# The last quarter of an output projection, computed token-major instead of feature-major

## The chip, the cores and the metric

One NeuronCore of a Trainium2 chip runs the whole program. The metric is the device time of one execution in microseconds (us). TensorE (PE in the profile) multiplies, with its weight loads shown apart (PEld); VectorE is DVE, ScalarE is ACT, GpSimd is POOL, and SyncE (SP) issues most DMAs. Each of these works through its own queue in the order of its program.

## The reference

One decoder layer over 512 tokens of 2,048 features. The part around the change:

```
mix = (g_a * y_a + g_b * y_b) @ w_o[l]
x = x + gt_a * mix
h = _rmsnorm(x, norm_ffn[l]) * (1.0 + sc_f) + sh_f
gate, up = jnp.split(h @ w_gate_up[l], 2, axis=-1)
```

`gt_a`, `sc_f` and `sh_f` are vectors of 2,048 features. The norm needs the sum over all features of x squared for each token, so no column of `h` can be formed before the last quarter of `mix @ w_o` is in x.

## The kernel before, in words

Every float32 operand is kept as a rounded part ("hi") and the rest ("lo"), and each product takes three matmuls: hi by hi, hi by lo, lo by hi. Weights arrive by DMA as "raw" tiles of 128x1024; ScalarE casts each to hi (L270) and VectorE subtracts to get lo (L271). There are five buffers for hi and five for lo, so a cast must wait until TensorE is done with the unit of weights five places earlier.

The work is a list of units (`Unit`, L37), each a piece of weights and the matmuls that use it. `Driver.run` (L113) takes them in order and issues their matmuls. It also counts matmuls by weight, and each time 12 are counted (`GROUP`, L34) it pumps: each generator in `drv.chains` (a chain of follow-up work, such as an epilogue) takes one step. `yield n` in a chain skips n - 1 pumps. `drv.hold()` at the end of a set costs one pump. TensorE, GpSimd and SyncE keep the order in which the program issues. On VectorE and ScalarE the order is set by a scheduler when the program is built, and it is then as fixed as the others.

All matmuls are recorded under L157, so tiles name them. Four stages matter, in this order:

- **The w_o product.** Columns 1024 to 1535 (`wo2`) come first, feature-major: a weight piece is stationary and all 512 tokens move. Columns 0 to 1023 come next by a Strassen scheme (`strassen_wo`), token-major. Its `finish` (L1448) multiplies each 128x512 tile by a gate row, adds x, stores the sum to `z_dram`, transposes it on TensorE (`zT`), copies it out of PSUM with ScalarE (L1471) and adds its squares to a running sum (`squares`, L1335: a Square on ScalarE, an add on GpSimd or VectorE).
- **The last quarter** (`half_sets`, L1530, called at L1763), columns 1536 to 2047, feature-major in two halves of 256 tokens. The first half goes through all 16 rows of weight tiles, then the second half does so again with weights loaded and split anew. Each matmul has a 128x128 weight piece as stationary operand and 256 tokens moving. A unit is 24 matmuls; a half is 8 units, 192 matmuls. At a half's end `wo_half_done` (L1520) adds gate times PSUM to the feature-major x (four instructions of 128x256 for a half's two tiles, L1329), squares, and starts `turned_x2` (L1504), which transposes the sums (`x2T`) and stores them to `z_dram`.
- **The norm** (`h2_gen`, L1786), one chain per half of the tokens. `part_rstd` (L1345) reduces the sum of squares on TensorE (`hss`), takes the reciprocal root on VectorE (tiles `rs`, then `diag`), and `spread` brings it to all partitions on TensorE (`hbc`). Then for each of eight pairs of feature tiles (q = 0 to 7) VectorE scales (L1795, two instructions), ScalarE shifts (L1796, two), ScalarE casts (L244, `h2h`) and VectorE subtracts (L247, `h2l`). The chain of the first half is started at the end of the last quarter's first half; its `hss` stands after 32 matmuls of the second half.
- **The first part of w_gate_up** (`gu0`), token-major, again in two halves of 256 tokens. A unit is 12 matmuls of 512 columns and uses one q. The first half's 96 matmuls use q = 0 to 7 of the first half of tokens, and meanwhile the norm's chain for the second half runs: its `hss` stands after 28 of those 96 matmuls, its `hbc` after 64.

In what follows v0 to v7 are the units of the last quarter's second half, and g0 to g7 those of gu0's first half.

Of the kernel before, what the change touches and what calls it, by code (L numbers as in the profile page):

```python
# [12 lines left out]
ALU = mybir.AluOpType  # L13
AX = mybir.AxisListType

P = 128
# [3 lines left out]
KT = 16  # L20
# [153 lines left out]
def block_kernel(ctx: ExitStack, tc: tile.TileContext, a: dict, out):  # L174
    nc = Core(tc, PINNED)
# [16 lines left out]
    def S(s, dt=F32):  # L192
        return slots.tile([P, 512], dt, tag="s", name=nm(s))

    def PS(s):
        return psum.tile([P, 512], F32, tag="ps", name=nm(s))
# [4 lines left out]
    def load(dst, src):  # L201
        nc.sync.dma_start(dst, src)

    def side(dst, src):
        nc.gpsimd.dma_start(dst, src)
# [6 lines left out]
    def tok(j):  # L212
        return slice(j * P, (j + 1) * P)
# [784 lines left out]
    chains = {}  # L998
# [318 lines left out]
    def load_x2(qs):  # L1317
        for q in qs:
            for h in range(2):
                x2[h][q] = S("x2")  # L1320
                load(x2[h][q][:].rearrange("p (k n) -> p k n", k=2),
                     a["xT"][256 * q:256 * q + 256, 256 * h:256 * h + 256].rearrange("(k p) n -> p k n", p=P))
# [12 lines left out]
    def squares(q, seg, eng):  # L1335

        s = S("sq")
        st = sums.setdefault(seg, [])
        nc.scalar.activation(view(s, seg), view(x2[seg[0]][q], seg), AF.Square)
        if st and eng is not None:  # L1340
            eng.tensor_tensor(view(st[0], seg), view(st[0], seg), view(s, seg), ALU.add)
        else:
            st.append(s)
# [79 lines left out]
    def strassen_wo():  # L1423
# [69 lines left out]
        def back(h):  # L1493
            for f in range(2):
                for t in range(2):
                    xk[h, t, f] = S("xk")
                    load(xk[h, t, f][:], a["x"][0, P * (2 * h + t):P * (2 * h + t) + P, 512 * f:512 * f + 512])

        with_pre([us[9]], gates)
        with_pre([us[12]], lambda: back(0))  # L1500
        with_pre([us[14]], lambda: (back(1), load_x2((6, 7))))
        return us

    def turned_x2(h, n):  # L1504
# [15 lines left out]
    def wo_half_done(n):  # L1520
        def done(h, ps):
            for j in range(4):
                k = 4 * n + j
                add_gated(h, k, ps[j // 2][:, 256 * (j % 2):256 * (j % 2) + 256], gt_mix)
                if j % 2:
                    squares(k // 2, HALF[h], nc.vector)
            drv.add(turned_x2(h, n))
        return done

    def half_sets(name, loads, x, done):  # L1530

        st = [None, None]

        def unit(h, k0):
            box = {}

            def start():
                box["raw"] = fetch(loads(k0, 2), 512, 2)

            def split():  # L1540
                box["w"] = halves(box.pop("raw"), 512, 2)

            def pre():
                if k0 == 0:
                    st[h] = [PS(name) for _ in range(2)]

            def one(kk, j, n, wi, xi):
                k = k0 + kk
                mm(st[h][j // 2][:, 256 * (j % 2):256 * (j % 2) + 256], box["w"][wi][:, kk, tok(j)],
                   x(k)[xi][:, 256 * h:256 * h + 256], start=k == 0 and j % 2 == 0 and n == 0,  # L1550
                   stop=k == KT - 1 and n == 2, skip_group_check=True)

            mms = [lambda kk=kk, j=j, n=n, wi=wi, xi=xi: one(kk, j, n, wi, xi)
                   for kk in range(2) for j in range(4) for n, (wi, xi) in enumerate(((0, 0), (0, 1), (1, 0)))]

            def post():
                if k0 + 2 == KT:
                    done(h, st[h])
                    st[h] = None
                    drv.hold()  # L1560

            return Unit(start, split, mms, pre, post, alone=True)

        return [[unit(h, k0) for k0 in range(0, KT, 2)] for h in range(2)]
# [55 lines left out]
    def with_pre(units, fn):  # L1620
        u = units[0]
        p0 = u.pre

        def pre():
            fn()
            if p0 is not None:
                p0()
        u.pre = pre
        return units
# [30 lines left out]
    def mixing():  # L1660
# [99 lines left out]

        def more():
            drv.ahead = LOADS
        first, second = half_sets("wo3", lambda k0, nk: loads(k0, nk, 3), mv, wo_half_done(3))  # L1763

        def half0():
            drv.finish(chains["act"])
            start_h2(0)()
        yield from with_pre(first, more) + with_pre(second, half0)


    def half_of(tile_, k):
# [13 lines left out]

    def h2_gen(h):  # L1786

        yield 3 if h else 1
        diag = part_rstd([HALF[h]])
        yield 6 if h else 4  # L1790
        r = spread(*diag)
        for q in range(8):
            f = S("h2f")
            for k in (2 * q, 2 * q + 1):
                nc.vector.scalar_tensor_tensor(half_of(f, k), half_of(x2[h][q], k), s_ffn[:, k:k + 1], r, op0=ALU.mult, op1=ALU.mult)  # L1795
                nc.scalar.activation(half_of(f, k), half_of(f, k), AF.Identity, bias=sh_ffn[:, k:k + 1])  # L1796
            x2[h][q] = None
            h2f[h][q] = f
            h2T[h][q] = hilo(f[:], "h2")
            h2n[h] = 2 * q + 2  # L1800
            yield 2
# [821 lines left out]
```

## Time and profile before

| What | us |
|---|---|
| Median of three runs | 2712.14 |
| Lowest, highest of the three | 2709.2, 2715.04 |
| The profiled execution's own time | 2706.44 |
| Its span, first to last instruction | 2704.6 |
| Mean granted TensorE clock | 0.999 of full |
| TensorE busy | 2683.6 |
| VectorE busy | 2087.6 |
| ScalarE busy | 1201.6 |

How to read it: the profile is of one execution, so sums are made against its 2706.44 us, 5.70 us under the median. Matmuls are pipelined: the recorded length of one (0.28 or 0.39 us) is longer than the time from its start to the next start, and it is the latter that adds up. A row of the timeline gives start, length, engine, line, operation, output and inputs, the count where equal rows were merged, and in brackets the engine's idle time before it and what ended that.

### The profile page before, as it was taken

The page shows a single profiled execution, that of the slowest core. Times are in us where ns is not written, and L with a number is a line of the kernel's source. Part 1 is how long each engine was busy: PE and PEld are TensorE (multiplying, and loading weights), DVE is VectorE, ACT ScalarE, POOL GpSimd, SP SyncE. Part 2 cuts the span into 40 slices and gives each one's busy share as a digit, 9 for nine tenths or more (in the row PEclk, how much of TensorE's full clock was granted, in tenths as well). Part 3 has the DMA queues.
Part 4 walks back from the last instruction along what each step waited for, and adds up shares of the span by engine and source line. Part 5 has one row for each costly group of instructions (what it writes and reads, how often), then busy time and mean ns, then how long its engine had stood idle before and what let it go on. Part 6 is the DMA issues. An engine that isn't in the chain of part 4 may idle for free.

```text
span 2704.6 us, 36528 instructions
## 1 busy us (share of the span) xinstructions
PE 2683.6 (99%) x13046; PEld 2237.3 (83%) x13046; DVE 2087.6 (77%) x3230; ACT 1201.6 (44%) x1720; POOL 228.6 (8%) x310
## 2 busy tenths in 40 slices
PE   9999999999999999999999999999999999999998
PEld 7888788888888888888888888888888888888886
DVE  8785666777768866768788778788878888788786
ACT  3443432453245333234574444444444446545454
POOL 0000002011100000000010000001101101011012
PEclk9999999999999999999999999999999999999999
DMA  9897565646664867854763566567767777788595
GB/s 372 306 351 268 158 192 177 201 152 191 187 172 136 286 223 285 306 187 134 272 193 120 193 209 208 202 218 250 243 227 263 252 249 212 210 238 226 179 278 154
DMA packets 312126, 600.45 MB, mean 222 GB/s; under 512 B 42852, under 2 KB 69636, under 8 KB 311816
## 3 DMA queue, kind: packets, MB, share of 16 engines
q1 hardware_dynamic: 257160, 486.52, 54.7%
q0 software_dynamic: 21888, 59.83, 8.3%
q10 hardware_dynamic: 32896, 51.78, 5.2%
q8 instruction: 102, 1.67, 0.3%
q14 instruction: 80, 0.66, 0.1%
HBM read 507.80 MB, written 90.20 MB: 221 GB/s over the span
## 4 chain that ended last, share of the span: by engine, by line
PE 98%; DVE 1%; ACT 1%; issue 0%; DMA 0%; SPq 0%; DVEq 0%; ACTq 0%
PE m L157 43%; PE gb L157 6%; PE v L157 4%; PE z L157 3%; PE ya L157 3%; PE ga L157 3%; PE k L157 3%; PE s L157 3%; PE q L157 3%; PE yb L157 3%; PE wo L157 3%; PE gu L157 3%; PE dn L157 2%; PE qk L157 2%; PE dnt L157 2%; PE ckv L157 2%
## 5 line engine op out<-in xcount | busy, mean ns | idle before, releaser
L1888 ACT CAST hi<-raws 128x1024 fp32r<-128x1024 f32 (+1 forms) x360 | 322.9, 907 | 575.3 <-DVE raws L1868 346.9
L1895 DVE TENSOR_TENSOR lo<-raws,hi 128x1024 fp32r<-128x1024 f32 (+1 forms) x360 | 376.0, 1046 | 176.5 <-ACT hi L1888 168.9
L270 ACT CAST hi<-raw 128x1024 fp32r<-128x1024 f32 x262 | 271.9, 1041 | 489.8 <-DMA raw<-in_w_in_dram 130.7
L271 DVE TENSOR_TENSOR lo<-raw,hi 128x1024 fp32r<-128x1024 f32 x262 | 320.7, 1227 | 190.2 <-ACT hi L270 183.6
L442 DVE CUSTOM_DVE_ANT_0 rawm<-rawm,cbc 128x1024 f32<-128x1024 f32 x192 | 233.9, 1234 | 3.8 <-DMA rawm<-in_w_mod_dram 3.5
L157 PE MATMUL m<-hi,h2h 128*128 128x512 f32 x480 | 190.7, 397 | 0.0
L157 PE MATMUL m<-hi,h2l 128*128 128x512 f32 x480 | 187.4, 390 | 0.0
L157 PE MATMUL m<-lo,h2h 128*128 128x512 f32 x480 | 186.9, 389 | 0.0
L157 PE MATMUL m<-hi,xh 128*128 128x512 f32 x448 | 174.6, 390 | 0.7 <-DVE al L247 0.7
L157 PE MATMUL m<-hi,xl 128*128 128x512 f32 x448 | 174.4, 389 | 0.0
L157 PE MATMUL m<-lo,xh 128*128 128x512 f32 x448 | 174.4, 389 | 0.0
L1895 DVE TENSOR_TENSOR lo<-sums,hi 128x1024 fp32r<-128x1024 f32 x120 | 146.7, 1222 | 22.2 <-ACT hi L1888 22.1
L1868 DVE TENSOR_TENSOR sums<-raws,raws 128x1024 f32<-128x1024 f32 x120 | 146.2, 1219 | 3.6 <-DMA raws<-in_w_down_dram 3.6
L1888 ACT CAST hi<-sums 128x1024 fp32r<-128x1024 f32 x120 | 126.1, 1051 | 36.1 <-PE m L157 22.5
L157 PEld LDWEIGHTS m<-hi,h2l 128*128 128x128 f32 x480 | 90.1, 188 | 19.4
L157 PEld LDWEIGHTS m<-lo,h2h 128*128 128x128 f32 x480 | 90.4, 188 | 17.8
L157 PEld LDWEIGHTS m<-hi,h2h 128*128 128x128 f32 x480 | 90.2, 188 | 17.3
L157 PE MATMUL gb<-hh,hi 128*128 128x512 f32 x256 | 102.4, 400 | 0.0
L157 PE MATMUL gb<-hh,lo 128*128 128x512 f32 x256 | 100.0, 391 | 0.0
L157 PE MATMUL gb<-hl,hi 128*128 128x512 f32 x256 | 99.9, 390 | 0.0
L157 PEld LDWEIGHTS m<-hi,xh 128*128 128x128 f32 x448 | 84.1, 188 | 18.8 <-DVE al L247 1.1
L157 PEld LDWEIGHTS m<-hi,xl 128*128 128x128 f32 x448 | 84.1, 188 | 17.6
(587 smaller groups left out, 6844.5 us busy)
## 6 DMA issues: line engine op xcount, KB each, us to landing
raws<-in_w_gate_up_dram SPq DMA_DIRECT2D x400, 256.0 KB, 4.0
rawm<-in_w_mod_dram SPq DMA_DIRECT2D x192, 512.0 KB, 5.5
raw<-in_w_in_dram SPq DMA_DIRECT2D x144, 512.0 KB, 5.0
raws<-in_w_down_dram SPq DMA_DIRECT2D x160, 256.0 KB, 5.2
s_dram<-raws ACTq DMA_DIRECT2D x88, 256.0 KB, 3.5
raws<-s_dram SPq DMA_DIRECT2D x88, 256.0 KB, 4.3
rawa<-in_w_in_dram SPq DMA_DIRECT2D x32, 512.0 KB, 5.6
raw<-in_w_o_dram SPq DMA_DIRECT2D x24, 512.0 KB, 6.9
```

The lines of the kernel that those rows point to most:

```text
L157: return self.tc.keep_in_program_order(f(*args, **kwargs))
L270: nc.scalar.copy(hi[:], raw[:])
L271: (lo_eng or nc.vector).tensor_tensor(lo[:], raw[:], hi[:].bitcast(F32), ALU.subtract)
L442: r = nc.vector.tensor_tensor_reduce(raw, raw, c, 1.0, 0.0, ALU.mult, ALU.add, parts[:, k, half:half + 1])
L1868: add = lambda o, x, y: behind(nc.vector.tensor_tensor(o, x, y, ALU.add))
L1888: nc.scalar.copy(hi[:], src)
L1895: nc.vector.tensor_tensor(lo[:], src, hi[:].bitcast(F32), ALU.subtract)
```

## The change

The two halves of the last quarter become two token-major sets (`tm_set` with two token tiles each). Now the mix tiles (128 features by 128 tokens) are stationary and 512 weight columns move. A unit has 12 matmuls of 512 columns, counted with weight 2, so that pumps come every 6 matmuls. The gate is a row, loaded by GpSimd's queue at the fifth unit of the first half. The x that is added is loaded token-major at the fifth unit of each half, as two tiles; the four loads of feature-major x (`load_x2((6, 7))`) at the end of the Strassen product go. At a half's end VectorE multiplies both PSUM tiles by the row; then a chain adds x, stores to `z_dram`, and three pumps later transposes, copies and squares q 6, a pump later q 7. The norm's chain steps past this chain's end before it reduces, and then waits 4 pumps for both halves instead of 4 and 6.

```diff
         with_pre([us[12]], lambda: back(0))
-        with_pre([us[14]], lambda: (back(1), load_x2((6, 7))))
+        with_pre([us[14]], lambda: back(1))
...
-        first, second = half_sets("wo3", lambda k0, nk: loads(k0, nk, 3), mv, wo_half_done(3))
+        row3, x3 = [], {}
+
+        def ready3(h):
+            for t in (2 * h, 2 * h + 1):
+                x3[t] = S("xk")
+                load(x3[t][:], a["x"][0, tok(t), 1536:2048])
+            if h == 0:
+                row3.append(S("row"))
+                side(row3[0][:], m_dram[1536:2048].partition_broadcast(P))
+
+        def half_done(h):
+            def done(ps):
+                ys = []
+                for t in (2 * h, 2 * h + 1):
+                    y = S("y")
+                    nc.vector.tensor_tensor(y[:], ps.pop(t)[:], row3[0][:], ALU.mult)
+                    ys.append(y)
...
+                def gen():
+                    for t in range(2):
+                        nc.vector.tensor_tensor(ys[t][:], ys[t][:], x3.pop(2 * h + t)[:], ALU.add)
+                        nc.scalar.dma_start(z_dram[2 * h + t, :, 1536:2048], ys[t][:])
+                    yield 3
+                    for q in (6, 7):
+                        ps = PS("zT")
+                        for j in range(2):
+                            for t in range(2):
+                                nc.tensor.transpose(ps[:, 256 * j + P * t:256 * j + P * t + P], ys[t][:, tok(2 * (q % 2) + j)], ident)
...
+                        x2[h][q] = S("x2")
+                        nc.scalar.copy(x2[h][q][:], ps[:])
+                        squares(q, HALF[h], nc.vector)
+                        ps = None
+                        yield
+                chains["last", h] = drv.add(gen())
+            return done
+
+        sets = [tm_set("wo3", lambda k0, nk: loads(k0, nk, 3), KT, mv, half_done(h), ts=(2 * h, 2 * h + 1), alone=True, weight=2)
+                for h in range(2)]
...
-        yield from with_pre(first, more) + with_pre(second, half0)
+        with_pre([sets[0][4]], lambda: ready3(0))
+        with_pre([sets[1][4]], lambda: ready3(1))
+        yield from with_pre(sets[0], more) + with_pre(sets[1], half0)
...
     def h2_gen(h):
-        yield 3 if h else 1
+        yield
+        while chains["last", h] in drv.chains:
+            yield
+
         diag = part_rstd([HALF[h]])
-        yield 6 if h else 4
+        yield 4
```

On TensorE's queue the counts that matter are these. In the second half of the last quarter, the transpositions of q 6 and q 7 stand after 28 and 34 of the 96 matmuls, `hss` after 40 and `hbc` after 64; before, `hss` and `hbc` stood after 32 and 80 of 192 matmuls of half the width. In gu0's first half, the transpositions stand after 28 and 34, `hss` after 40 and `hbc` after 64.

The first place is VectorE's queue at the end of the last quarter's first half, before. `lo` is the split of a weight unit, `sq` the sum of squares that `hss` reads, `rs` the reciprocal root.

```order
L1329 SCALAR_TENSOR_TENSOR x_2033_11505<-wo_2047_11573,gt_mix,x_2033_11505 128x256 x2
L1329 SCALAR_TENSOR_TENSOR x_2035_11509<-wo_2048_11574,gt_mix,x_2035_11509 128x256 x2
L271 TENSOR_TENSOR lo_12016<-raw_11819,hi_12015 128x1024
L1341 TENSOR_TENSOR sq_10880<-sq_10880,sq_11903 128x512
L1341 TENSOR_TENSOR sq_10880<-sq_10880,sq_11908 128x512
L403 TENSOR_SCALAR rs_11982<-hss_11977 128x2
```

The same place on VectorE's queue in the changed kernel; the four `lo` are those of v4, v5, v6 and v7.

```order
L1785 TENSOR_TENSOR y_11805<-y_11805,xk_11675 128x512
L271 TENSOR_TENSOR lo_11870<-raw_11745,hi_11869 128x1024
L271 TENSOR_TENSOR lo_11910<-raw_11773,hi_11909 128x1024
L271 TENSOR_TENSOR lo_11955<-raw_11833,hi_11954 128x1024
L1341 TENSOR_TENSOR sq_10880<-sq_10880,sq_11888 128x512
L271 TENSOR_TENSOR lo_11974<-raw_11855,hi_11973 128x1024
L1341 TENSOR_TENSOR sq_10880<-sq_10880,sq_11904 128x512
L403 TENSOR_SCALAR rs_11925<-hss_11920 128x2
```

The last add of squares has moved behind the split of v7.

The second place is TensorE's queue in gu0's first half, before: `x2T` are the transpositions for the store, `hss` the second half's reduction.

```order
L157 MATMUL gu_2155_12276<-hi_12277,h2h_12165 128x512
L157 MATMUL x2T_12344<-kc,x_2034_11507 128x128 x2
L157 MATMUL x2T_12344<-kc,x_2036_11511 128x128 x2
L157 MATMUL hss_12352<-ones,sq_10882 128x1 x4
L157 MATMUL gu_2155_12276<-lo_12278,h2h_12165 128x512
```

The same place on TensorE's queue in the changed kernel, from the last transposition of q 7 on.

```order
L157 MATMUL zT_12161<-kc,y_12061 128x128
L157 MATMUL gu_2152_12064<-lo_12066,h2h_12047 128x512
L157 MATMUL gu_2152_12064<-hi_12065,h2l_12048 128x512
L157 MATMUL gu_2151_12063<-hi_12097,h2h_12087 128x512
L157 MATMUL gu_2151_12063<-lo_12098,h2h_12087 128x512
L157 MATMUL gu_2151_12063<-hi_12097,h2l_12088 128x512
L157 MATMUL gu_2152_12064<-hi_12097,h2h_12087 128x512
L157 MATMUL hss_12184<-ones,sq_10882 128x1 x4
```

`hss` now depends on transpositions that stand six matmuls ahead of it; before, it did not depend on the transpositions beside it.

The third place is VectorE's queue during the same stage, before, from the gated sums of the second half on.

```order
L1329 SCALAR_TENSOR_TENSOR x_2036_11511<-wo_2102_11932,gt_mix,x_2036_11511 128x256 x2
L247 TENSOR_TENSOR h2l_12246<-h2f_12240,h2h_12245 128x512
L1795 SCALAR_TENSOR_TENSOR h2f_12294<-x_1795_10351,s_ffn,hbc_12078 128x256
L1341 TENSOR_TENSOR sq_10882<-sq_10882,sq_12267 128x512
L1795 SCALAR_TENSOR_TENSOR h2f_12294<-x_1795_10351,s_ffn,hbc_12078 128x256
L1341 TENSOR_TENSOR sq_10882<-sq_10882,sq_12272 128x512
```

The same place on VectorE's queue in the changed kernel, from the add of x on (the two multiplications by the row and the scaling of q 3 stand ahead of it).

```order
L1785 TENSOR_TENSOR y_12061<-y_12061,xk_11952 128x512
L271 TENSOR_TENSOR lo_12174<-raw_12035,hi_12173 128x1024
L247 TENSOR_TENSOR h2l_12088<-h2f_12082,h2h_12087 128x512
L1841 SCALAR_TENSOR_TENSOR h2f_12114<-x_1793_10347,s_ffn,hbc_11984 128x256 x2
L271 TENSOR_TENSOR lo_12224<-raw_12069,hi_12223 128x1024
L271 TENSOR_TENSOR lo_12252<-raw_12101,hi_12251 128x1024
L247 TENSOR_TENSOR h2l_12120<-h2f_12114,h2h_12119 128x512
L1841 SCALAR_TENSOR_TENSOR h2f_12152<-x_1795_10351,s_ffn,hbc_11984 128x256 x2
L1341 TENSOR_TENSOR sq_10882<-sq_10882,sq_12143 128x512
L247 TENSOR_TENSOR h2l_12158<-h2f_12152,h2h_12157 128x512
L1341 TENSOR_TENSOR sq_10882<-sq_10882,sq_12168 128x512
```

Between the gated sums and the last add of squares there are now three weight splits (`lo` of g5, g6 and g7), two scalings (q 4 and q 5) and three `h2l` (q 3, q 4 and q 5).

More of the change, by code (lines that the diff above doesn't have):

```diff
@@ L1762, in more @@
             drv.ahead = LOADS
-        first, second = half_sets("wo3", lambda k0, nk: loads(k0, nk, 3), mv, wo_half_done(3))
+        row3, x3 = [], {}
[13 more added lines that the diff above has]
+                    ys.append(y)
+                if h:
+                    row3.clear()
+                def gen():
[8 more added lines that the diff above has]
+                                nc.tensor.transpose(ps[:, 256 * j + P * t:256 * j + P * t + P], ys[t][:, tok(2 * (q % 2) + j)], ident)
+                        if q % 2:
+                            ys.clear()
+                        x2[h][q] = S("x2")
[7 more added lines that the diff above has]
+                for h in range(2)]
         def half0():
```

## The prediction

> **What bounds the kernel now.** I read the page first: the span, the busy times and the chain that ended last.
>
> ```profile
> span 2704.6 us, 36528 instructions
> PE 2683.6 (99%) x13046; PEld 2237.3 (83%) x13046; DVE 2087.6 (77%) x3230; ACT 1201.6 (44%) x1720; POOL 228.6 (8%) x310
> PE 98%; DVE 1%; ACT 1%; issue 0%; DMA 0%; SPq 0%; DVEq 0%; ACTq 0%
> ```
>
> TensorE is busy for all but 21 us and is 98% of the chain. So a us saved on TensorE's queue is a us saved, and a us in which it waits is lost: no slack elsewhere takes it up. Next I cut the time into the four stages that the change can reach. The rows are the last quarter's first half and second half, then gu0's first and second half; columns are the stretch, its length, and the busy time and count of PE, PEld, DVE, ACT and POOL, then clock, DMA share and GB/s.
>
> ```profile
> 1331.58:1357.21 25.63, 25.63 (x218) 25.63 (x216) 22.19 (x24) 16.46 (x22) 8.45 (x5) 1.00 0.93 332
> 1357.21:1384.06 26.85, 26.35 (x221) 26.09 (x220) 21.04 (x39) 18.37 (x28) 4.54 (x4) 1.00 0.62 191
> 1384.06:1408.03 23.97, 23.97 (x116) 19.83 (x115) 22.02 (x44) 18.81 (x30) 0.00 (x0) 1.00 0.61 189
> 1408.03:1431.40 23.37, 23.03 (x100) 17.61 (x99) 19.70 (x30) 19.39 (x31) 0.56 (x1) 1.00 0.61 190
> ```
>
> VectorE is busy for 21.04 of 26.85 us and for 22.02 of 23.97 us in the second and third stretch, where the norm's chain runs. It is the next bound there: what the change puts in front of TensorE in those two stretches has to pass VectorE with 1.95 us to spare in the third.
>
> **The matmuls.** The chain that ended last, in order of time, gives start, length and count of runs of matmuls: 512 columns feature-major, 512 columns in the Strassen product, 256 columns in the last quarter, and four transpositions.
>
> ```profile
> 1210.14 43.52 PE wo L157 x192
> ...
> 1305.78 4.11 PE m L157 x18
> ...
> 1339.32 5.76 PE wo L157 x48
> ...
> 1345.08 0.44 PE zT L157 x4
> ```
>
> A matmul of 256 columns takes 5.76 / 48 = 0.120 us, one of 512 takes 43.52 / 192 = 0.2267 us (in the Strassen rows 0.228). 384 of the first go, 46.08 us; 192 of the second come, 43.52 us. That is -2.56 us, or -2.2 us at 0.228. I take -2.56, since the 192 are of the same product. The transpositions stay ten groups in the last quarter and two in gu0's first half: nothing. [...]
>
> **Loads.** Four loads of feature-major x go, four of token-major x come, with one more row. Landing times by issue line:
>
> ```profile
> xk<-in_x_dram SPq DMA_DIRECT2D x8, 256.0 KB, 4.8
> row<-m_dram POOLq DMA_DIRECT2D x1, 256.0 KB, 5.4
> ```
>
> Both are issued at the fifth unit of a half, so four units before use: 48 x 0.2267 = 10.9 us against 5.4. On SyncE's queue they pass the weights of v2 and later, and of g2 and later, which are due more than 10 us on. I cost them at nothing; without that cover the multiplication or add would wait 5 us.
>
> **The first new wait.** `hss` of the first half waits for the last add of squares. TensorE's rows around it before (bracket: idle, and what ended it), and `hbc` in gu0 with the matmul behind it:
>
> ```profile
> 1361.79 0.28 PE L157 MATMUL wo<-ml,hi 128*128 128x256 f32 x1
> 1362.57 1.05 PE L157 MATMUL hss<-ones,sq 128*128 128x1 f32 x8 [0.50 <-DVE sq L1341]
> ...
> 1400.42 0.70 PE L157 MATMUL hbc<-diag,ones 128*128 128x256 f32 x2
> 1400.77 0.58 PE L157 MATMUL gu<-lo,h2h 128*128 128x512 f32 x1
> ```
>
> Without a wait `hss` would have started 0.12 us after 1361.79; it lost 0.66 us. ScalarE's rows (copy out of PSUM, square; a weight cast that waited for TensorE, two shifts, `h2h`), then VectorE's (two adds of squares beside GpSimd, gated sums, two multiplications by a row, two adds of x, scalings, `h2l`, a split, an add of squares):
>
> ```profile
> 1359.30 0.56 ACT L1471 COPY x<-zT 128x512 f32<-128x512 f32 x1
> 1359.90 0.63 ACT L1339 ACTIVATE sq<-x 128x512 f32<-128x512 f32 x1
> ...
> 1384.14 1.05 ACT L270 CAST hi<-raw 128x1024 fp32r<-128x1024 f32 x1 [0.37 <-PE wo L157]
> 1385.09 0.90 ACT L1796 ACTIVATE h2f<-h2f,sh_ffn 128x256 f32<-128x256 f32 x2
> 1386.03 0.62 ACT L244 CAST h2h<-h2f 128x512 fp32r<-128x512 f32 x1
> ```
>
> ```profile
> 1328.87 1.28 DVE L1440 TENSOR_TENSOR y<-m,row 128x512 f32<-128x512 f32 x2
> 1330.06 1.28 DVE L1459 TENSOR_TENSOR y<-y,xk 128x512 f32<-128x512 f32 x2
> ...
> 1356.69 1.66 DVE L1329 SCALAR_TENSOR_TENSOR x<-wo,gt_mix,x 128x256 f32<-128x256 f32 x4 [0.28 <-PE wo L157]
> ...
> 1359.94 2.58 DVE L1341 TENSOR_TENSOR sq<-sq,sq 128x512 f32<-128x512 f32 x2
> ...
> 1371.66 0.87 DVE L1795 SCALAR_TENSOR_TENSOR h2f<-x,s_ffn,hbc 128x256 f32<-128x256 f32 x2
> ...
> 1375.44 0.87 DVE L1795 SCALAR_TENSOR_TENSOR h2f<-x,s_ffn,hbc 128x256 f32<-128x256 f32 x2
> ...
> 1378.70 0.87 DVE L1795 SCALAR_TENSOR_TENSOR h2f<-x,s_ffn,hbc 128x256 f32<-128x256 f32 x2
> ...
> 1381.04 0.69 DVE L247 TENSOR_TENSOR h2l<-h2f,h2h 128x512 fp32r<-128x512 f32 x1 [0.34 <-ACT h2h L244]
> 1381.65 0.86 DVE L1795 SCALAR_TENSOR_TENSOR h2f<-x,s_ffn,hbc 128x256 f32<-128x256 f32 x2
> 1382.44 1.22 DVE L271 TENSOR_TENSOR lo<-raw,hi 128x1024 fp32r<-128x1024 f32 x1
> ...
> 1387.75 0.68 DVE L1341 TENSOR_TENSOR sq<-sq,sq 128x512 f32<-128x512 f32 x1
> ```
>
> Now the last add stands behind the split of v7, whose cast waits for TensorE to end v2, the 36th matmul; `hss` comes after the 40th. From the end of v2: 0.4 us until the copy of q 7 frees ScalarE (part of its 0.56), cast 1.05, split 1.22, add 0.68, together 3.35 us. TensorE fills 4 x 0.2267 = 0.91 us of it. The wait is 2.4 us, against 0.66 before. Lower bound: with the split out of the way, copy, square and add (1.87 us) behind the last transposition, less six matmuls (1.36): 0.5. Upper: the add beside GpSimd, where two took 2.58 us instead of 1.36: 3.6. I take 2.4, since the queue leaves no other order.
>
> Behind it, the root and `diag` must be ready when `hbc` comes, 24 matmuls or 5.44 us later:
>
> ```profile
> 1363.66 0.16 DVE L403 TENSOR_SCALAR rs<-hss 128x2 f32<-128x2 f32 x1 [1.14 <-PE hss L157]
> ...
> 1367.89 0.47 DVE L1364 TENSOR_SCALAR diag<-kc,rs 128x128 f32<-128x128 f32 x2
> ```
>
> That took 4.7 us with two splits of 1.22 us in between, which no longer stand there: it is hidden.
>
> **The second new wait.** `hss` in gu0 waits for the second half's last add of squares, which stands on VectorE behind three splits, two scalings and three `h2l`. I count from the end of v4, since the split of g1 waits for its buffers and the first scaling stands behind that split.
>
> VectorE's way: cast and split of g1, 1.05 + 1.22 = 2.27 us. Three q at the pace of the rows 1371.66 to 1381.65: 9.99. Then by starts of neighbouring rows: two multiplications 1.2, scaling of q 3 0.8, two adds 1.2, three splits 3.6, three `h2l` at 0.61 1.8, two scalings 1.6, two adds of squares 1.3; together 11.5. To that, 1.5 us in which VectorE waits for ScalarE (an estimate: cast, shifts and `h2h` take 1.05 + 0.90 + 0.62 us per q, and q 6's copy and square stand behind the `h2h` of q 4, q 7's behind that of q 5). Sum 25.3 us.
>
> TensorE's way: 36 matmuls to the half's end 8.16, `hbc` 0.35, 40 matmuls of gu0 9.07, two groups of transpositions 0.88; 18.5 us.
>
> The wait is 6.8 us, where there was none. Lower bound: no waits on ScalarE (-1.5) and every q at the last cycle, 2.95 us (-1.1): 4.2. Upper: 2.3 us more, as if two of the three splits each waited out a cast: 9.1. I take 6.8, by the measured pace.
>
> What else goes or comes is in these counts: four gated sums per half, 1.66 us, go from VectorE; 2.4 us of multiplications and adds come. What is late next, in gu0's second half, is already late before:
>
> ```profile
> 1417.83 0.51 PE L157 MATMUL gu<-hi,h2l 128*128 128x512 f32 x1 [0.34 <-DVE h2l L247]
> ```
>
> The rest of the norm's chain keeps the same distance to TensorE as before, so I take nothing for it, -0.5 to +0.5.
>
> **The sum.** -2.56 - 0.66 + 2.4 + 6.8 = +6.0 us. The bounds give +1.5 (-2.56 - 0.66 + 0.5 + 4.2) to +10.3 (-2.2 - 0.66 + 3.6 + 9.1 + 0.5). The profiled execution's own 2706.44 becomes 2712.4 (span 2710.6), and the median 2712.14 becomes 2718.1. About 0.2%, 5.4 us, is what a measurement of this kernel can tell from no change, so the forecast lies just beyond that bound.
>
> **The rivals.** *The squares come in time: faster.* If VectorE's way from v4 to the last add is not longer than TensorE's 18.5 us, and the first wait falls too, only -2.56 - 0.66 = -3.2 us is left: 2708.9. For it speaks that before no wait is recorded at `hss` in gu0. Against it: VectorE would have to lose 6.8 of 25.3 us, while its rows there stand nearly end to end. It decides from 18.5 us on.
>
> *The waits come, but half as long*, because VectorE enters gu0 further ahead than I count: the sum is near its lower end, +1.5 to +4, say 2714.9. For it: my start, g1's split, is tied to TensorE, but earlier scalings could pass quicker once TensorE stands still.
>
> *The clock falls in the second wait.* After the last matmuls of the program the trace shows this (stretches of 1 us; the clock is the column behind the busy times):
>
> ```profile
> 2694.00:2695.00 1.00, 0.26 (x2) 0.00 (x0) 0.77 (x2) 0.89 (x2) 0.00 (x0) 1.00 1.01 371
> ...
> 2698.00:2699.00 1.00, 0.00 (x0) 0.00 (x0) 0.96 (x3) 0.86 (x2) 0.00 (x0) 0.79 0.03 6
> 2699.00:2700.00 1.00, 0.00 (x0) 0.00 (x0) 0.56 (x1) 0.48 (x1) 0.00 (x0) 0.50 0.91 344
> ```
>
> TensorE ends at 2694.26 and the granted clock halves at 2698.58 (0.79 is 0.42 us at half), 4.3 us later. A wait of over 4.3 us could do the same. The price I take from the program's first matmuls, though their clock is recorded as full: 14 of 512 columns between 5.1 and 9.9 us,
>
> ```profile
> L157 PE MATMUL warm<-wide,ones_r x14: 392/628/796, 5.1 to 9.9; 128*128 128x512 f32 x14
> ```
>
> so 4.8 / 13 = 0.369 us each, 1.9 us more than at 0.2267. The sum is then +7.9: 2720.0. [...]
>
> **How the numbers follow.** Forecast 0.45; clock falls as well 0.23; waits half as long 0.20; squares in time 0.12. The median of three runs moves by up to 2.9 us, so the forecast's own range is 2714 to 2722. The range 2711 to 2723 holds it, the clock's case and the short waits, and leaves out the faster rival and the tails. Beyond 5.4 us slower: 0.27 of the forecast, 0.20 of the clock's case, 0.03 of the short waits, 0.50. Faster by more than 5.4 us: 0.03 from the rival and the spread of runs. Within: 0.47.
>
> **What would show it.** Right: two waits of TensorE at `hss`, ended by the add of squares (L1341), near 2.4 and 6.8 us; the last quarter 0.5 to 1.0 us shorter over both halves, gu0's first half 6 to 7 us longer; and a granted clock of 1.00 or, by the third rival, under 1.00 behind the second wait. Wrong: waits under 1 us at both `hss`, matmuls of 512 columns in the last quarter away from 0.2267 us, a wait for the row or x, or idle time later than gu0 that was not there.

## The result, and the profile after

The changed kernel took 2719.9 us, median of 6 runs (2718.72 to 2724.23), beside 2710.78 for the kernel before (6 runs, 2706.83 to 2715.04). The ratio is 1.0037, 95% interval 1.0027 to 1.0047: slower by 0.37%, about 10 us, which is more than the 0.2% that a measurement can tell. The profiled execution took 2720.32 us. Two executions of the kernel before that were run beside e1 to e4 were slow ones (2980.17 and 5512.83 us); they are in its median given below, but in no ratio.

First the head of the page of the kernel after: span and busy times.

```profile
span 2718.2 us, 36150 instructions
PE 2689.5 (99%) x12854; PEld 2232.5 (82%) x12854; DVE 2088.0 (77%) x3230; ACT 1202.5 (44%) x1720; POOL 234.2 (9%) x311
```

TensorE has 192 matmuls fewer and is busy for 5.9 us more: that can't be work, and points to the clock. The four stages of the prediction, with the columns it explains:

```profile
1334.96:1359.60 24.64, 24.64 (x123) 20.36 (x122) 19.77 (x23) 14.93 (x20) 13.95 (x6) 1.00 0.97 337
1359.60:1388.58 28.98, 26.89 (x123) 22.03 (x122) 19.24 (x32) 15.57 (x22) 4.70 (x4) 0.94 0.59 183
1388.58:1421.60 33.02, 26.80 (x111) 21.73 (x110) 25.98 (x51) 21.01 (x36) 0.00 (x0) 0.84 0.44 133
1421.60:1445.00 23.40, 23.33 (x103) 18.20 (x102) 20.00 (x30) 20.08 (x32) 0.56 (x1) 1.00 0.63 195
```

Against the same stages before, the first, in which only the matmuls' form and the loads changed, is 0.99 us shorter (24.64 for 25.63). The second is 2.13 longer, the third 9.05 longer, the fourth unchanged (23.40 for 23.37). In the two that are longer the clock is at 0.94 and 0.84. TensorE's rows at the two places:

```profile
1370.28 0.40 PE L157 MATMUL wo<-hi,mh 128*128 128x512 f32 x1
1372.77 1.05 PE L157 MATMUL hss<-ones,sq 128*128 128x1 f32 x8 [2.09 <-DVE sq L1341]
...
1398.75 0.40 PE L157 MATMUL gu<-hi,h2h 128*128 128x512 f32 x1
1405.19 1.84 PE L157 MATMUL hss<-ones,sq 128*128 128x1 f32 x8 [6.05 <-DVE sq L1341]
```

Both `hss` wait for the add of squares (L1341). From where `hss` could have started, 0.23 us behind the matmul ahead of it, they lose 2.26 and 6.21 us. What ran ahead of them: for the first, the cast and split of v7 and the last add; for the second, the `h2h` of the other half's norm, the copy of q 7 and the last add.

```profile
1369.81 1.05 ACT L270 CAST hi<-raw 128x1024 fp32r<-128x1024 f32 x1
1370.89 1.22 DVE L271 TENSOR_TENSOR lo<-raw,hi 128x1024 fp32r<-128x1024 f32 x1 [1.24 <-ACT hi L270]
1372.03 0.68 DVE L1341 TENSOR_TENSOR sq<-sq,sq 128x512 f32<-128x512 f32 x1
...
1402.56 0.62 ACT L244 CAST h2h<-h2f 128x512 fp32r<-128x512 f32 x1
1403.08 0.58 ACT L1796 COPY x<-zT 128x512 f32<-128x512 f32 x1
1404.35 0.69 DVE L1341 TENSOR_TENSOR sq<-sq,sq 128x512 f32<-128x512 f32 x1 [0.45 <-ACT sq L1339]
```

The clock behind the two waits, in stretches of 1 and 2 us, and two matmuls of the first fall:

```profile
1373.00:1374.00 1.00, 1.00 (x9) 0.96 (x9) 0.14 (x1) 0.00 (x0) 0.00 (x0) 1.00 0.57 144
1374.00:1375.00 1.00, 1.00 (x5) 0.81 (x4) 0.83 (x6) 0.00 (x0) 0.00 (x0) 0.82 1.01 353
1375.00:1376.00 1.00, 1.00 (x3) 0.75 (x3) 0.81 (x6) 0.00 (x0) 0.00 (x0) 0.50 0.08 27
...
1402.00:1404.00 2.00, 0.00 (x0) 0.00 (x0) 1.26 (x2) 1.94 (x5) 0.00 (x0) 0.50 0.83 228
1410.00:1412.00 2.00, 2.00 (x6) 1.59 (x5) 0.49 (x2) 1.87 (x4) 0.00 (x0) 0.50 0.00 0
1412.00:1414.00 2.00, 2.00 (x9) 1.59 (x9) 2.00 (x3) 0.50 (x1) 0.00 (x0) 0.95 0.00 0
```

```profile
1375.18 0.63 PE L157 MATMUL wo<-hi,mh 128*128 128x512 f32 x1
1375.61 0.63 PE L157 MATMUL wo<-lo,mh 128*128 128x512 f32 x1
```

The clock halves twice: for 3.4 us from 1374.6 on, when TensorE is already working again, and for 10.2 us from 1401.9 on, of which TensorE works 6.9. At half clock a matmul of 512 columns takes 0.43 us (1375.18 to 1375.61) instead of 0.2267, so nearly half of the working time is lost: about 1.6 and 3.3 us.

The profiled executions differ by 13.9 us, the medians by 9.1. Part of that lies where nothing was changed: the first matmul of the last quarter starts 3.45 us later than in the kernel before (1335.03 for 1331.58). In the changed kernel's execution the clock also halved twice far ahead of it, for 3.4 us each, which the kernel before's execution doesn't show:

```profile
12.00:16.00 4.00, 3.21 (x8) 2.43 (x8) 3.90 (x10) 1.21 (x2) 0.00 (x0) 0.59 1.03 420
772.00:776.00 4.00, 2.70 (x10) 2.21 (x11) 3.20 (x8) 1.98 (x5) 0.00 (x0) 0.74 0.80 244
```

So below I compare runs by the **stretch**: from the first matmul of the last quarter to the first transposition of gu0's output (`guT`, in gu0's second half). It was 84.4 us before and 95.3 after.

### The profile page after: what moved, and what is told of

Same layout as the page of the kernel before. It is cut to its first block, busy times and chain, and to the rows that moved or that the text cites. A ratio compares the mean times of both kernels' runs of the same rounds, so it can differ in the third digit from the quotient of the medians.

```text
span 2718.2 us, 36150 instructions
## 1 busy us (share of the span) xinstructions
PE 2689.5 (99%) x12854; PEld 2232.5 (82%) x12854; DVE 2088.0 (77%) x3230; ACT 1202.5 (44%) x1720; POOL 234.2 (9%) x311
## 4 chain that ended last, share of the span: by engine, by line
PE 97%; DVE 1%; ACT 1%; DMA 0%; issue 0%; SPq 0%; DVEq 0%; ACTq 0%
PE m L157 43%; PE gb L157 6%; PE v L157 4%; PE z L157 3%; PE s L157 3%; PE ya L157 3%; PE k L157 3%; PE ga L157 3%; PE q L157 3%; PE yb L157 3%; PE wo L157 3%; PE gu L157 2%; PE dn L157 2%; PE qk L157 2%; PE dnt L157 2%; PE ckv L157 2%
## 5 line engine op out<-in xcount | busy, mean ns | idle before, releaser
L271 DVE TENSOR_TENSOR lo<-raw,hi 128x1024 fp32r<-128x1024 f32 x262 | 320.3, 1225 | 199.2 <-ACT hi L270 195.1
L157 PEld LDWEIGHTS m<-lo,xh 128*128 128x128 f32 x448 | 84.1, 188 | 17.7 <-DVE lo L1941 0.2
```

The lines of the kernel that those rows point to most:

```text
L157: return self.tc.keep_in_program_order(f(*args, **kwargs))
L271: (lo_eng or nc.vector).tensor_tensor(lo[:], raw[:], hi[:].bitcast(F32), ALU.subtract)
```

## The experiments

The theory at the start: the cost is the two waits and the falls of the clock behind them, and what is left of the change is a gain. Each kernel was timed in five rounds against the kernel before on the same chip. "Waits" are TensorE's idle times over 0.5 us in the stretch, with the tile that was waited for.

| Run | Median, us | Ratio to before (95%) | Stretch, us | Waits, us |
|---|---|---|---|---|
| e5_after | 2719.13 | 1.0029 (1.0019 to 1.0040) | 94.7 | hss 2.09, hss 6.06 |
| e1_fill | 2716.89 | 1.0023 (1.0014 to 1.0032) | 90.7 | none |
| e2_late0 | 2720.82 | 1.0037 (1.0024 to 1.0050) | 93.0 | h2h 1.66, hss 3.33, h2h 2.59 |
| e3_accum | 2705.37 | 0.9980 (0.9971 to 0.9989) | 81.4 | none |
| e4_poolsplit | 2727.33 | 1.0064 (1.0051 to 1.0077) | 100.5 | hss 2.09, zT 1.10, h2l 0.65, hss 7.34 |
| e6_accum1 | 2718.19 | 1.0024 (1.0014 to 1.0035) | 91.8 | hss 2.09, h2h 2.54 |
| e7_late1 | 2722.75 | 1.0041 (1.0028 to 1.0053) | 98.3 | hss 2.09, h2h 2.19, h2h 2.59 |
| e8_nosplit | 2718.03 | 1.0025 (1.0016 to 1.0035) | 92.4 | hss 2.09, hss 4.15 |
| e9_accum0 | 2714.87 | 1.0018 (1.0009 to 1.0026) | 91.0 | hss 6.09 |
| e10_accumlate | 2714.53 | 1.0013 (1.0004 to 1.0022) | 88.2 | h2h 2.50 |
| e11_lead | 2720.06 | 1.0034 (1.0021 to 1.0046) | 97.2 | hss 2.09, hss 6.34 |
| e12_early2 | 2712.09 | 1.0008 (0.9999 to 1.0017) | 86.9 | hss 3.65 |

The medians of before were 2710.26 (e1 to e4), 2710.73 (e5 to e8), 2710.26 (e9 to e11) and 2709.09 (e12).

**e5_after**, the changed kernel again, for comparison:

> The changed kernel itself, on the same chip as the three that follow, so that they can be compared with it. Both theories: 9 to 10 us over the kernel before (2719.9 against 2710.8), two waits at hss near 2.3 and 6.2 us, and a clock of one half for 3.4 us behind the first and for about 10 us behind the second.

The waits are the same to 0.01 us. The second fall of the clock lasted 6.8 us, not 10.2.

**e1_fill: the waits filled with work that nobody reads.**

```diff
+        ps = PS("fill")
+        for _ in range(28 if h else 10):
+            mm(ps[:], ones_r[:], (h2T[0][0][0] if h else mixT[15][0])[:], start=True, stop=True)
         diag = part_rstd([HALF[h]])
```

> The changed kernel, with 10 matmuls of 512 columns that nobody reads put on TensorE ahead of the first hss and 28 ahead of the second. At 0.2267 us each they take 2.27 and 6.35 us, about as long as the two waits (2.26 and 6.21 us), so TensorE is busy where it waited and nothing else is changed. The median before is 2710.8 us, and the changed kernel's 2719.9. Theory (two waits, and the clock falls behind them): the granted clock stays at 1.00 from the last quarter's second half to the end of gu0, the 1.7 and 3.4 us that the falls cost are saved, and the time is about 2714.8, 4 to 5 us over the kernel before. Rival (the waits alone cost, the clock does not matter): the time stays at about 2720, 9 us over. Rival (the 512-column form or its loads cost): 2720 as well, with the waits filled and other idle time to be seen.

Stretches of 10 us behind the two places, in e1_fill; the clock is the third column from the end:

```profile
1370.00:1380.00 10.00, 10.00 (x51) 8.25 (x50) 6.20 (x18) 3.70 (x5) 0.00 (x0) 1.00 0.53 159
1400.00:1410.00 10.00, 10.00 (x49) 8.25 (x48) 7.09 (x23) 5.12 (x9) 0.00 (x0) 1.00 0.37 108
```

The clock stays at 1.00, and the stretch is 4.1 to 4.6 us shorter than in the two runs of the changed kernel, though the filling is as long as the waits were. So the falls cost 4 to 5 us of the stretch, and the waits cause them. What is left is 6.3 us over before in the stretch. The medians show the gain less clearly: 6.6 us over before here, 8.4 and 9.1 us for the changed kernel, each beside its own runs of before, and 2716.89 lies 2 us over the expected 2714.8. Their intervals are too wide to tell 2 us from 4.

**e2_late0: the first `hss` 12 matmuls later.**

```diff
+        if h == 0:
+            yield 2
         diag = part_rstd([HALF[h]])
```

> The changed kernel with the first hss moved 12 matmuls (2.7 us) further back on TensorE; the second stays. Theory (a wait is as long as VectorE's queue is late at that place): the first wait of 2.26 us falls under 0.5 and the clock does not fall behind it, which saves 2.3 + 1.7 = 4.0; since TensorE is then up to 4 us earlier at gu0 while VectorE is not, the second wait grows by 1 to 3 us. Net 1 to 3 us under the changed kernel: 2717 to 2719. Rival (the place of hss is all that matters): 4 us under it, 2716, with the second wait as it was, 6.2 us. Rival (VectorE is the bound through both halves): all of the 2.3 us comes back at the second hss, and only the clock's 1.7 us or nothing is saved.

```profile
1394.72 0.50 PE L157 MATMUL gu<-hi,h2h 128*128 128x512 f32 x1 [1.66 <-ACT h2h L244]
...
1403.16 1.02 PE L157 MATMUL hss<-ones,sq 128*128 128x1 f32 x8 [3.33 <-DVE sq L1341]
...
1419.37 0.50 PE L157 MATMUL gu<-hi,h2h 128*128 128x512 f32 x1 [2.59 <-ACT h2h L244]
```

The first wait and its fall are gone, but the second `hss` still waits and two new waits stand at `h2h`, a scaled tile of gu0. 7.6 us of waits replace 8.1. The stretch is 1.7 to 2.3 us shorter, the times can't be told from the changed kernel's and miss the expected 2717 to 2719. What TensorE gains at the first place it waits for in gu0, though at other tiles than expected.

**e3_accum: row sums instead of squares of transposed tiles.** ScalarE's Square adds up each token's row as it goes; both reductions stand where the kernel before had them.

```diff
+    row_sums = [C(f"row_sums{h}", [P, 2]) for h in range(2)]
...
+        nc.vector.tensor_tensor(more[:], more[:], ps[:, 0:n], ALU.add)
+        y = token_rstd(more[:], n, 1.0 / D)
...
+                        nc.scalar.activation(S("sq")[:], ys[t][:], AF.Square, accum_out=row_sums[h][:, t:t + 1])
...
-                        squares(q, HALF[h], nc.vector)
...
-        yield
-        while chains["last", h] in drv.chains:
-            yield
-
-        diag = part_rstd([HALF[h]])
-        yield 4
+        yield 3 if h else 1
+        diag = part_rstd([HALF[h]], row_sums[h])
+        yield 6 if h else 4
```

> The changed kernel, but the squares of the last quarter are no longer taken from its transposed tiles: ScalarE squares the token-major sums and adds up each row as they are formed, and the two row sums are added to what hss gives. So hss needs only the first three quarters' squares, and it and hbc stand where the kernel before had them. The token-major form, its loads, transpositions and copies all stay. Theory (the cost is hss waiting for squares behind the transpositions): no wait over 1 us at hss, no fall of the clock there, and the gain of the wider matmuls is left, 192 x 0.2267 for 384 x 0.120 us, 2.56 us, less at most 1 us for later tiles: 2708 to 2709.5, against 2710.8 before. Rival (the token-major form or its loads cost time themselves): 2714 or more. Rival (VectorE is the bound in gu0's first half, whatever hss waits for): the wait moves to the scaled tiles of gu0 or to hbc and the time stays over 2714.

The stretch in three parts (both halves of the last quarter, then gu0 up to `guT`), and the two `hss`:

```profile
1334.20:1358.82 24.62, 24.62 (x122) 20.34 (x120) 21.70 (x26) 15.87 (x23) 16.29 (x6) 1.00 0.98 343
1358.82:1383.83 25.01, 25.01 (x123) 20.97 (x122) 21.13 (x40) 19.49 (x33) 4.81 (x4) 1.00 0.68 208
1383.83:1415.65 31.82, 31.82 (x149) 26.36 (x148) 27.67 (x53) 25.69 (x42) 0.00 (x0) 1.00 0.60 190
```

```profile
1363.34 0.95 PE L157 MATMUL hss<-ones,sq 128*128 128x1 f32 x8
...
1390.63 0.95 PE L157 MATMUL hss<-ones,sq 128*128 128x1 f32 x8
```

No idle time, a clock of 1.00, and a stretch 2.9 us shorter than before. This is the version that beats both kernels: 0.20% under before (0.11 to 0.29), and 2.6 us under the lower end of what was expected. So the token-major form, its loads and its transpositions cost nothing that shows; what costs is which squares the reduction reads, and the later place of `hss` and `hbc` that follows from it.

**e4_poolsplit: every other weight split of gu0 on GpSimd** (`lo_eng=True` for its sets).

> The changed kernel with the weight splits of every other unit of gu0 put on GpSimd, which takes them out of VectorE's queue around the second hss. Theory (the second wait is VectorE's queue, in which the splits of gu0's weights stand ahead of the last adds): the second wait falls from 6.2 us by 2 to 4 us, while the first stays at 2.3; 2715 to 2718 in all. Rival (the second wait is set by the chain of transposition, copy, square and add itself, not by what stands ahead on VectorE): still about 6 us, 2720. Splits on GpSimd could be slower than TensorE uses them; then waits for the split weights appear in gu0, and the run says less.

GpSimd's split, a small VectorE subtraction beside it, and `hss`:

```profile
1398.03 3.03 POOL L157 TENSOR_TENSOR lo<-raw,hi 128x1024 fp32r<-128x1024 f32 x1 [4.09 <-ACT hi L270]
```

```profile
1398.72 2.88 DVE L247 TENSOR_TENSOR h2l<-h2f,h2h 128x512 fp32r<-128x512 f32 x1
```

```profile
1409.73 1.84 PE L157 MATMUL hss<-ones,sq 128*128 128x1 f32 x8 [7.34 <-DVE sq L1341]
```

A miss: the wait grew. The subtraction took 2.88 us beside GpSimd's and 0.69 alone, which probably cost more than VectorE was relieved of; the run says nothing on its queue.

**e6_accum1: row sums in the second half alone.** The edits of e3_accum for h = 1; the first half as in the changed kernel.

> The changed kernel, with the row sums of e3_accum in the second half of the tokens alone: the second hss needs no transposed tiles and stands where the kernel before had it, the first stays as in the changed kernel. Theory (each wait costs its length and its own fall of the clock): the second wait, 6.2 us, and the 3.0 to 3.4 us of its clock go; the first, 2.3 us and 1.7 us, stays. From the stages: 2.56 gained, 0.5 gained, 2.26 + 1.7 lost, so about 1 us over the kernel before, and 8 to 9 us under the changed one. Rival (the second wait is only the first one's delay, passed on): 5 us or more over the kernel before, with a wait elsewhere in gu0's first half.

```profile
1371.31 1.05 PE L157 MATMUL hss<-ones,sq 128*128 128x1 f32 x8 [2.09 <-DVE sq L1341]
...
1406.33 0.69 PE L157 MATMUL gu<-hi,h2h 128*128 128x512 f32 x1 [2.54 <-ACT h2h L244]
```

The theory's 1 us over before was wrong; it is 6.5 us by the ratio. The second `hss` waits no more, but gu0 waits for `h2h` all the same, and the clock falls. The rival's figures came out. Its reason, that the second wait is the first one passed on, does not hold: e9_accum0 below has no first wait and still a second one of 6.09 us.

**e7_late1: the second `hss` 30 matmuls later.**

```diff
+        if h == 1:
+            yield 5
         diag = part_rstd([HALF[h]])
```

> The changed kernel with the second hss moved 30 matmuls (6.8 us) further back on TensorE, so that it stands behind 70 of the 96 in gu0's first half, and hbc behind 94. Theory (VectorE and ScalarE, taking turns in the norm's chain, are late in gu0 as a whole, as the waits for h2h of 1.66 and 2.59 us in e2_late0 say): the wait at hss goes, but two or three shorter ones come at h2h or h2l, and the second half's scaled tiles come too late for gu0's second half; -3 to +3 us against the changed kernel. Rival (only the place of hss matters): all of 6.2 and 3.0 us goes, 9 us under the changed kernel.

The wait at `hss` went, waits of 2.19 and 2.59 us at `h2h` came, and the stretch is 3.6 us longer than in e5_after: the direction of the theory, a little past its range. A later place for `hss` is no cure.

**e8_nosplit: gu0's weight splits left out in its first half** (the sets take the high part twice, `return hi, hi` ahead of L271).

> The changed kernel, with the low parts of gu0's weights left out in its first half: the high part stands in for them in the matmuls, so TensorE has the same work and VectorE has 8 subtractions of 128x1024 fewer, 8 x 1.22 us, five of which stand between 1387 and 1401 us in the changed kernel's VectorE queue ahead of the last add for hss. Theory (VectorE has no slack there, so the second wait is made of work that stands ahead in its queue): the second wait falls from 6.2 us to under 2, with the clock's fall smaller or gone, and the time is 5 to 9 us under the changed kernel. Rival (ScalarE's casts and copies are the bound, or the chain from transposition to add alone): the wait stays over 4 us and the time within 2 us of the changed kernel.

VectorE's rows of one step of the norm, and `hss`:

```profile
1385.83 0.86 DVE L1843 SCALAR_TENSOR_TENSOR h2f<-x,s_ffn,hbc 128x256 f32<-128x256 f32 x2
1388.06 0.69 DVE L247 TENSOR_TENSOR h2l<-h2f,h2h 128x512 fp32r<-128x512 f32 x1 [1.36 <-ACT h2h L244]
1388.67 0.86 DVE L1843 SCALAR_TENSOR_TENSOR h2f<-x,s_ffn,hbc 128x256 f32<-128x256 f32 x2
```

```profile
1404.39 1.84 PE L157 MATMUL hss<-ones,sq 128*128 128x1 f32 x8 [4.15 <-DVE sq L1343]
```

The second wait fell only from 6.06 to 4.15 us, and the time is 1.1 us under e5_after: here too the rival's figures came out. Without the splits VectorE idles 0.9 to 1.4 us in a step, waiting for ScalarE's `h2h`, and the step shown still takes 2.84 us (1385.83 to 1388.67). The two engines take turns: scaling on VectorE, shift and cast on ScalarE, subtraction on VectorE, and the next scaling stands behind that subtraction. In e3_accum, with the splits, a step takes 2.77 (four from 1371.30 to 1382.36). TensorE uses a tile pair in 12 x 0.2267 = 2.72 us. So the norm runs at about TensorE's own pace, and should not win back what distance it has lost. That gave a new theory, the *lead*: in the changed kernel `hbc` of the first half comes 7.7 us ahead of gu0 (1380.87 to 1388.58), where it came 13.9 us ahead before.

**e9_accum0: row sums in the first half alone**, so that the lead is 13.2 us again (1369.17 to 1382.34), with the second half's squares as in the changed kernel.

> The changed kernel, with the row sums of e3_accum in the first half of the tokens alone: the first hss and hbc stand where the kernel before had them; the second half's squares still come from its transposed tiles, and its hss stays behind 40 of gu0's 96 matmuls. New theory (lead): the second wait is the lead that the first half's norm has lost. Its hbc came 13.9 us ahead of gu0 before, 13.1 us in e3_accum, 7.7 us in the changed kernel and in e6_accum1, and behind it one pair of feature tiles takes VectorE and ScalarE in turn about 2.75 us, as long as TensorE needs for the 12 matmuls that use it, so a lost lead is never won back. With 13.1 us again the second wait falls from 6.05 to under 1.5 us and no clock falls: 2707 to 2709.5. Theory of before (each hss waits for its own half's squares): the second wait stays over 5 us with its fall of the clock, and the time is 5 to 7 us over the kernel before, 2716 to 2718.

```profile
1398.60 1.84 PE L157 MATMUL hss<-ones,sq 128*128 128x1 f32 x8 [6.09 <-DVE sq L1341]
```

```profile
1395.03 0.91 ACT L1850 ACTIVATE h2f<-h2f,sh_ffn 128x256 f32<-128x256 f32 x2 [1.22 <-DVE h2f L1849]
1395.96 0.62 ACT L244 CAST h2h<-h2f 128x512 fp32r<-128x512 f32 x1
1396.49 0.58 ACT L1804 COPY x<-zT 128x512 f32<-128x512 f32 x1
1397.10 0.63 ACT L1339 ACTIVATE sq<-x 128x512 f32<-128x512 f32 x1
```

As an account of the second wait the lead theory fell: 6.09 us, with the full lead. The time, 2714.87, lies between the two forecasts. ScalarE's rows show why: the copy of q 7 (L1804) stands behind the last shift and `h2h` of the other half's norm, and the shift waits for VectorE's scaling.

**e10_accumlate: e3_accum with the first `hbc` 24 matmuls later**, so that nothing waits for squares and only the lead is lost (`yield 6 if h else 8`).

> e3_accum, with only the first half's hbc moved 24 matmuls (5.4 us) further back, to where the changed kernel has it; no reduction waits for squares in either half. Theory (lead): 3 to 6 us of waits come back in gu0's first half, at h2h, h2l or the second hss or hbc, perhaps with a fall of the clock; 4 to 8 us over e3_accum, so 2709 to 2714. Theory of before (squares behind the transpositions): nothing waits, 2705 to 2706.5.

```profile
1392.52 0.95 PE L157 MATMUL hss<-ones,sq 128*128 128x1 f32 x8
...
1404.52 0.50 PE L157 MATMUL gu<-hi,h2h 128*128 128x512 f32 x1 [2.50 <-ACT h2h L244]
```

The stretch is 6.7 us longer than in e3_accum: the lost lead alone costs that, with waits that look like those of e6_accum1. (Its ratio is 0.0033 over that of e3_accum, about 9 us, of which 1.1 us are two waits just behind the stretch, 0.46 at `h2h` and 0.61 at `h2l`. The time is 0.5 us past the expected range.)

**e11_lead: the changed kernel with the first `hbc` 12 matmuls earlier** (`yield 4 if h else 2`).

> The changed kernel, with the first half's hbc 12 matmuls (2.7 us) earlier, 12 instead of 24 behind its hss. Theory (lead): the second wait falls from 6.05 to 3.4 to 4.2 us; for that TensorE may wait up to 1 us at hbc, since root and diag took 3.7 us from the start of hss; 1 to 3 us under the changed kernel, 2716.5 to 2718.5. Theory of before: the second wait stays at 6 us and the time at 2719 to 2720.

```profile
1379.00 0.76 PE L157 MATMUL hbc<-diag,ones 128*128 128x256 f32 x2
...
1406.50 1.84 PE L157 MATMUL hss<-ones,sq 128*128 128x1 f32 x8 [6.34 <-DVE sq L1341]
```

The lead theory failed here as well: the lead is 10.6 us, the wait 6.34. In the changed kernel 2.9 us more of lead don't shorten the second wait; it is set by the squares.

**e12_early2: e9_accum0 with the second half's transpositions 6 matmuls earlier**, `hss` staying.

```diff
-                    yield 3
+                    yield 2 if h else 3
                     for q in (6, 7):
...
+        if h:
+            yield 1
```

> e9_accum0 with the second half's transpositions 6 matmuls (1.36 us) earlier and its hss where it was, behind 40 matmuls of gu0. On ScalarE that moves one thing: the copy and square of q 7 now stand ahead of the last shift and h2h of the first half's norm, where they stood behind them. In e9_accum0 that copy started at 1396.49, though its transposition was over at 1391.1, and the add that hss waits for came 1.9 us behind the copy's end. Theory (the second wait with a full lead is ScalarE's queue, in which the copies take turns with the norm of the other half): the copy follows the square of q 6 at once, about 2.7 us earlier, the second wait falls from 6.1 to 3 to 3.8 us, and the time is 2 to 4 us under e9_accum0: 2711 to 2713. Rival (VectorE's splits and adds hold it, or the transpositions come too late): the wait stays at 5.5 to 6.1 us and the time at 2714.5 to 2715.5.

```profile
1393.48 0.63 ACT L1339 ACTIVATE sq<-x 128x512 f32<-128x512 f32 x1
1394.02 0.57 ACT L1804 COPY x<-zT 128x512 f32<-128x512 f32 x1
1394.61 0.63 ACT L1339 ACTIVATE sq<-x 128x512 f32<-128x512 f32 x1
1395.33 0.91 ACT L1852 ACTIVATE h2f<-h2f,sh_ffn 128x256 f32<-128x256 f32 x2
```

```profile
1396.43 1.02 PE L157 MATMUL hss<-ones,sq 128*128 128x1 f32 x8 [3.65 <-DVE sq L1341]
```

The copy now follows the square of q 6 at once, and the wait falls by 2.44 us, as expected; the stretch is 4.1 us shorter, the rest being a shorter fall of the clock. So 2.4 of the 6.1 us of the second wait with a full lead are the order on ScalarE. What holds the other 3.65 is not tested. The trace shows the copy of q 6 late there too: its transposition began at 1387.61, the copy at 1392.87, with an `h2h` (1391.36) and a weight cast (1391.92) just ahead of it. (The 1.9 us that the expectation gives run from the start of that copy to the end of the add, 1396.49 to 1398.45, not from the copy's end.)

**Together.** Two things are wrong in gu0's first half, and each alone is enough to stop TensorE: the squares of the second half stand behind the norm of the first on ScalarE (e9_accum0: 9.6 us over e3_accum in the stretch), and the first half's norm has lost its lead (e10_accumlate: 6.7 us). Their costs don't add up, as the time from gu0's first matmul to `guT` shows: 41.2 and 41.8 us in the two runs of the changed kernel, 41.4 with the lead restored (e9_accum0), 38.2 with the squares out of the way (e6_accum1), 31.8 with both (e3_accum). So curing the lead alone gave nothing in gu0, curing the squares alone 3.0 to 3.6 us, and both 9.4 to 9.9. The 3.8 to 4.3 us that e9_accum0 gains in the whole stretch are the first wait and its fall of the clock, which its edit also removes.

## Why the prediction was right, and where not

The direction and the cause were right, and the size was near: 2718.1 was forecast, 2719.9 measured, within 2711 to 2723. That the two lie 1.8 us apart is partly luck. The forecast was +6.0 us on a median of 2712.14 from three runs; six runs put that median at 2710.78, and the change at +9.1 us. What the forecast left out is the clock, which it had as a rival with a chance of 0.23. Two of its signs failed for that reason: the last quarter became 1.1 us longer over both halves, not 0.5 to 1.0 shorter, and gu0's first half 9.05 us longer, not 6 to 7. By its steps:

- **Matmuls, -2.56.** Right within 0.4 us. The first half, in which only the loads changed as well, is 0.99 us shorter, where half of 2.56 is 1.28; in e3_accum both together are 2.85 shorter (49.63 for 52.48), against -2.56 and the old wait's -0.66.
- **First wait, 2.4.** 2.26 measured. The queue that the prediction read, from the end of v2 over cast and split to the add, is the one that the trace shows (cast 1369.81, split 1370.89, add 1372.03). Root and `diag` were hidden: no wait at `hbc`.
- **Second wait, 6.8.** 6.21 measured and 0.17 at the transpositions, 6.4 together. The sum fits the rows: from the end of v4 (1379.96) to the end of the last add (1405.04) they take 25.1 us where 25.3 was worked out, and VectorE idles 1.5 us in the part for which 1.5 was taken. What the sum doesn't tell is which of its terms would shorten the wait. It holds 3.6 us for three splits, yet leaving all the splits out took 1.9 us off the wait (e8_nosplit), since they fill times in which VectorE otherwise waits for ScalarE; changing the place of one copy on ScalarE took 2.4 off the wait of e9_accum0 (e12_early2). In the changed kernel too the copy of q 7 stands on ScalarE right behind an `h2h` of the other half's norm (1402.56, 1403.08), but no run moved it there. So VectorE's queue alone is not the bound; the turn-taking of the two engines fits what the runs show.
- **gu0's second half and the loads, nothing.** Right: 23.40 for 23.37 us, and no wait for row or x.
- **The sum, +6.0.** With the clock kept up (e1_fill) the stretch is 6.3 us over before. That is the forecast as it was meant.
- **The clock.** Here a size was off. The rival "The clock falls in the second wait" had one fall, at 1.9 us, and let waits of over 4.3 us decide. There were two falls: the first wait of 2.26 us was enough. They cost 4.9 us by the rows, 4.1 to 4.6 by e1_fill. The price per matmul was low as well: 0.369 us was taken from the program's first matmuls, 0.43 is what one took at half clock. Forecast and rival with 5 us instead of 1.9 give +11, which is the stretch's 10.3 to 10.9 us; the medians give 8 to 9.
- **"Squares in time", 2708.9**, was what the form is worth if the reduction doesn't wait: e3_accum is that kernel, 2.9 us shorter in the stretch where -3.2 was worked out.

One thing is open. In the medians e3_accum gains 4.9 us and the changed kernel loses 9.1, each 1 to 2 us better than by its stretch. Some 1 us lies behind the stretch (from `guT` to the end of the span 1288.65 us before, 1287.65 in e3_accum); the other may come from the profiled execution of before, which at 2706.44 was under its median. No run tells.

## What to carry to other kernels

When a step that ends in a reduction changes its form, look at which tiles the reduction reads, and take the sum from the form that comes first (here the token-major rows) instead of the transposed copies. A chain that runs at the same pace as the engine it feeds keeps its delays, so its head start can be worth as much as its speed (6.7 us in e10_accumlate). Where two causes each suffice for a wait, curing one can show almost nothing, so cure both before judging either. Price a wait of TensorE like those here (2.09 us and longer) with a possible fall of the clock behind it, and test that price by filling the wait with matmuls that nobody reads.

## What was not expected of the hardware

The clock fell for 3.4 us (to 0.50 in the changed kernel, from 1375 to 1378 us) behind waits of 2.09 us with a reduction of one-column matmuls behind them (0.95 us in e3_accum), and this in every profile that has this wait: both of the changed kernel, e4_poolsplit, e6_accum1, e7_late1, e8_nosplit and e11_lead; in e4_poolsplit, e7_late1 and e11_lead it lasted 6.8 us. Behind waits of 1.66 and 2.59 us at `h2h` in e2_late0 it did not fall (1.00 from 1390 to 1400 us and from 1410 to 1440 us; between them it fell behind the 3.33 us at `hss`), behind 2.19 and 2.59 us in e7_late1, 2.50 in e10_accumlate and 2.54 in e6_accum1 it did. A wait of 3.65 us cost one such time of 3.4 us in e12_early2, 6.09 us three (10.2 us) in e9_accum0, 6.06 us two (6.8 us) in e5_after. No run shows what decides how many of these times a wait costs.

A GpSimd subtraction of 128x1024 took 2.41 to 3.03 us where VectorE's takes 1.22, and a VectorE subtraction beside it took up to 2.88 us for 0.69. A Square on ScalarE with its row sum took 0.61 to 0.62 us and 0.19 more for reading the sum, where the plain one took 0.63.
